# Seven block products for all columns of both output projections

## The chip, the cores and the metric

The kernel runs on one core of a Trainium2 chip. The metric is device time in microseconds (us): the median of three runs of the same program was 2065.28 us (2064.89 to 2066.32). A profile of one more execution shows what each engine did: PE is the matrix engine (PEld its weight loads), DVE the vector engine, ACT the scalar engine, POOL the general engine, SP the engine that issues most plain loads. Partition means one of the 128 rows of on-chip memory; PSUM is the memory that matrix products are summed in, in banks of 128 x 512 numbers.

## The reference

Two residual layers over x (512 tokens x 2048 columns, float32):

```
x = x + (attention(norm(x)) * silu(gate)) @ da_w_out      # layer 0, 8 heads
x = x + (rwkv(norm(x))      * silu(gate)) @ rw_w_out      # layer 1, 32 heads in 16 pairs
```

Both output projections are matrix products of 512 x 2048 by 2048 x 2048. This case is about these two alone. Every product is done in float32 precision by three passes: each factor is split into a high part (a cast) and a low part (the rest), and high x high, high x low and low x high are summed (`mm3`, L116).

## The kernel before

**Tiling.** K (the 2048 channels that are summed over) has 16 tiles of 128, the tokens 4 tiles of 128, the output columns 4 blocks of 512. One product (one instruction of PE) takes a 128 x 128 tile of the activations and a 128 x 512 tile of the weights. The activations of one K tile are a "row" (128 channels x 512 tokens); `split_row` (L471) casts it on ACT (L475) and takes the low part on DVE (L476). `split_w` (L92) does the same for weights, one K tile at a time: ACT L109, DVE L110. High and low weight tiles have four buffers each, raw weights (two K tiles, 512 KB) three, named wraw.

**Order.** The program is written as one sequence; a planner orders it for each engine by priority and by when it takes things to be ready, and inserts the waits. `split_w` runs at a raised priority, the chains below at a higher one. Each engine, and each queue of transfers, then works strictly in its order. Transfers issued by SP are plain loads; those that add into on-chip memory are issued by POOL.

**Output stage of layer 0.** Column blocks 0 and 1 are plain (`unit_tok`, L184): for each pair of K tiles, 2 x 4 token tiles x 3 passes = 24 products. Beside block 0 the last head's attention still runs. It is a `Chain`: a sequence of steps that `tick` (L168) advances by one whenever a given number of products has been issued. Its last step makes the last two rows (K tiles 14 and 15); `feed` loads and splits the other rows a little ahead of their use. The attention of one 128-token block is scores, `turn` (transposition), `weigh`, `turn_y`; four blocks overlap. Beside block 1, `sum_forms` (L758) loads rows of the first 12 K tiles again and makes four sums of them (below).

Column blocks 2 and 3 go through `seven` (L793). It takes 12 of the 16 K tiles as two halves of 6, the tokens as two halves of 256 and the columns as two blocks of 512, and does the 2 x 2 x 2 block product by seven block products in place of eight (the scheme of Strassen and Winograd). Each block product is 3 groups of two K tiles, 12 products a group, 36 in all. It needs sums of activations (S1 to S4, made by `sum_forms`) and sums of weights. The weights are summed in place: `add_w` (L788) lets POOL issue a transfer that adds another block's weights to the ones on the chip, once they are split. Three such tiles, Ts, live through the whole function: 11 uses them first, then S1, S2 and 22. The weights of S4 (b22) are changed in place in the same way for S3. The remaining 4 K tiles are added plainly (`plain`).

The order of `seven` is 11, 12, plain pairs on the first columns, S1, first plain pair on the second columns, S2, S4, second plain pair on the second columns, S3, 22. The banks are named X (11, S2, S3), y and z. The residual x is loaded by SP before the sums; `take` (L824) adds a bank to it on DVE (L827; in the plain blocks L1058 and L1852).

**Output stage of layer 1.** The same, from L1804 on. Beside block 0 run the scan of the last head pair (steps of 4, 4 and 5 products) and the end of the pair before. After the scan come `outputs` (L1671, L1675: tile Y), `centre`, `normal` (L1696 to L1704), and `finish_y` (four transpositions, L1716, and L1718), then the gate (L1592) and the split of row 15. Row 14 comes from the pair before.

Of the kernel before, what the change touches and what calls it, by code (L numbers as in the profile page):

```python
# [13 lines left out]
F32 = mybir.dt.float32  # L14
# [9 lines left out]
P = 128  # L24
# [728 lines left out]
NS = 6  # L753
KG = 2
PLACES = {"11": (0, 0), "12": (0, 1), "21": (1, 0), "22": (1, 1)}


def sum_forms(g, src, i, rows, homes):  # L758


    nc = g.nc
    for r, k0 in zip(rows, (i * KG, NS + i * KG)):
        nc.gpsimd.dma_start(out=r, in_=src[k0 * P : (k0 + KG) * P, :].rearrange("(k p) t -> p k t", p=P))
    (a, b), (c, d) = [(r[:, :, 0:256], r[:, :, 256:512]) for r in rows]
    out = {}
    for nm, o, x, y, op in (("S1", d, b, d, ALU.subtract), ("S3", b, a, b, ALU.subtract),
                            ("S2", d, d, a, ALU.subtract), ("S4", c, c, d, ALU.add)):
        with g.tc.issue_after(g.rowsplit):
            nc.vector.tensor_tensor(out=o, in0=x, in1=y, op=op)
        tags = homes[i][nm]  # L770
        n = KG if len(tags) < 2 * KG else 1
        if len(tags) == 1:
            pool, t, m = tags[0]
            both = pool.tile([P, 2, n, 256], F32R, name="f" + nm, tag=t, bufs=m)
            at = [both[:, 0], both[:, 1]]
        else:
            at = [x[0].tile([P, n, 256], F32R, name="f" + nm, tag=x[1], bufs=x[2])[:] if type(x) is tuple else x
                  for x in tags]
        out[nm] = []
        for x in range(KG // n):  # L780
            hi, lo, v = at[2 * x], at[2 * x + 1], o[:, x * n : (x + 1) * n]
            nc.scalar.copy(hi, v)
            nc.vector.tensor_sub(lo, v, hi.bitcast(F32))
            out[nm] += [(hi[:, k], lo[:, k]) for k in range(n)]
    return out
# [7 lines left out]
def seven(g, w, load, rows, sums, c1, c2, acc, Ts, banks, done, begin=None):  # L793
# [3 lines left out]
    nc = g.nc  # L797

    def products(out, lhs, wt, first, end):
        for k in range(KG):  # L800
            for t in range(2):
                aH, aL = lhs(k, t)
                mm3(nc, out[t][:], aH, aL, wt[0][:, k, :], wt[1][:, k, :], first and k == 0, end and k == KG - 1,
                    g, True)

    def block(k0, t0):
        return lambda k, t: [x[:, t0 + t * P : t0 + (t + 1) * P] for x in rows[k0 + k]]

    def prod(out, i, form, raw, first=False, end=False):
        wt = split_w(g, None, KG, 512, 0, raw)  # L810
        if form in PLACES:
            t, kb = PLACES[form]
            lhs = block(kb * NS + i * KG, t * 256)
        else:
            lhs = lambda k, t: [x[:, t * P : (t + 1) * P] for x in sums[i][form][k]]
        products(out, lhs, wt, first, end)

    def plain(i, c, *outs):
        k0 = 2 * NS + i * KG
        wt = split_w(g, None, KG, 512, 0, load(k0, c))  # L820
        for out, t0, first, end in outs:
            products(out, block(k0, t0), wt, first, end)

    def take(nm, ps, op=ALU.add):  # L824
        with g.tc.high_priority(offset=SCAN):
            for t in range(2):
                nc.vector.tensor_tensor(out=acc[nm][t], in0=acc[nm][t], in1=ps[t][:], op=op)  # L827

    N = NS // KG
    last = N - 1  # L830
    X, y, z = banks(0), banks(1), banks(2)
    for i in range(N):
        load_w(g, Ts[i], w[c1 // 512], i * KG, slice(0, KG))
# [1100 lines left out]
```

## Time and profile before

| | us |
|---|---|
| median of 3 runs | 2065.28 (2064.89 to 2066.32) |
| the profiled execution | 2065.58 |
| its span, first to last instruction | 2063.5 |
| PE busy | 2048.4 (99%) |
| DVE busy | 1676.3 (81%) |
| ACT busy | 1276.0 (62%) |
| POOL busy | 417.8 (20%) |

An instruction's row has its start and its length in us, the engine, the line of the kernel (L118 is line 118), the operation, the tiles out<-in, and in square brackets how long the engine was idle before it and what ended that. A row of a stretch has its borders, its length, and each engine's busy time. Matrix products overlap in the profile: one lasts 0.39 us, but the next starts earlier. Issuing, branch and semaphore instructions do not count as busy.

### The profile page before, as it was taken

Reading aid. Unit: us, or ns where it says so; the run is one execution under the profiler, and the core shown is the slowest. Engines: PE = TensorE matmul, PEld = TensorE weight load, DVE = VectorE, ACT = ScalarE, POOL = GpSimd, SP = SyncE. Lnnn points to the kernel's source line nnn. Section 1 sums busy time; section 2 is a strip of 40 time slices with the busy share of each in tenths; the row PEclk is TensorE's granted clock in tenths of the full one; section 3 lists DMA queues with packets and bytes.
Section 4 is the critical chain, followed back from the end, with each engine's and each line's share of the span. In section 5 each row is a group of like instructions: output and inputs, shape, how many; then the busy total and the mean of one; then the engine's idle time right before and its main releaser. Section 6 shows DMA issues by size and latency. Waiting matters only on the chain. (4 is left out here: it accounts for less than half of the span.)

```text
span 2063.5 us, 35254 instructions
## 1 busy us (share of the span) xinstructions
PE 2048.4 (99%) x11924; PEld 1689.0 (82%) x11924; DVE 1676.3 (81%) x4379; ACT 1276.0 (62%) x3043; POOL 417.8 (20%) x733
## 2 busy tenths in 40 slices
PE   9999999999999999999999999999999999999999
PEld 8878878888888888888778888888888888877887
DVE  5979798897978976576878888888888888887745
ACT  5667676776767754455666666666666666665433
POOL 0020211202111000101233322222333213232001
PEclk9999999999999999999999999999999999999999
DMA  6387877869688665742222222222222222244665
GB/s 203 114 166 184 167 169 167 179 172 177 172 161 217 171 200 187 179 114 95 75 75 70 82 77 81 76 87 75 78 76 80 70 89 74 84 134 151 214 165 121
DMA packets 100773, 269.70 MB, mean 131 GB/s; under 512 B 12432, under 2 KB 28960, under 8 KB 100592
## 3 DMA queue, kind: packets, MB, share of 16 engines
q1 hardware_dynamic: 62016, 173.21, 26.3%
q0 software_dynamic: 24144, 78.23, 20.8%
q10 hardware_dynamic: 14432, 16.01, 2.2%
q8 instruction: 94, 1.54, 0.3%
q14 instruction: 87, 0.71, 0.1%
HBM read 251.41 MB, written 15.99 MB: 130 GB/s over the span
## 5 line engine op out<-in xcount | busy, mean ns | idle before, releaser
L118 PE MATMUL pp<-hH,wh 128*128 128x512 f32 x1024 | 416.6, 407 | 0.0
L118 PE MATMUL pp<-hL,wh 128*128 128x512 f32 x1024 | 411.9, 402 | 0.0
L118 PE MATMUL pp<-hH,wl 128*128 128x512 f32 x1024 | 411.7, 402 | 0.0
L109 ACT CAST wh<-wraw 128x512 fp32r<-128x512 f32 (+1 forms) x412 | 254.3, 618 | 221.7 <-PE pp L118 128.8
L110 DVE TENSOR_TENSOR wl<-wraw,wh 128x512 fp32r<-128x512 f32 (+1 forms) x412 | 292.6, 711 | 83.2 <-ACT wh L109 77.7
L118 PE MATMUL pp<-wh,hH 128*128 128x512 f32 x820 | 325.1, 397 | 0.4 <-DVE G L382 0.4
L118 PE MATMUL pp<-wl,hH 128*128 128x512 f32 x820 | 321.8, 392 | 0.6 <-DVE wl L616 0.6
L118 PE MATMUL pp<-wh,hL 128*128 128x512 f32 x820 | 321.3, 392 | 0.0
L118 PEld LDWEIGHTS pp<-hH,wh 128*128 128x128 f32 x1024 | 192.8, 188 | 38.0 <-issue 2.1
L118 PEld LDWEIGHTS pp<-hH,wl 128*128 128x128 f32 x1024 | 193.1, 189 | 33.2
L118 PEld LDWEIGHTS pp<-hL,wh 128*128 128x128 f32 x1024 | 193.1, 189 | 31.4
L118 PE MATMUL pp<-wh,S 128*128 128x512 f32 x672 | 214.5, 394 | 0.0
L615 ACT CAST wh<-T 128x512 fp32r<-128x512 f32 x224 | 137.1, 621 | 94.2 <-PE pp L118 71.0
L118 PEld LDWEIGHTS pp<-wh,hH 128*128 128x128 f32 x820 | 154.0, 188 | 32.3 <-issue 0.6
L118 PEld LDWEIGHTS pp<-wh,hL 128*128 128x128 f32 x820 | 154.5, 188 | 31.4
L1633 POOL COPY SA<-VS 64x64 f32<-64x64 f32 x224 | 75.1, 335 | 518.2 <-DVE VS L1651 464.6
L118 PEld LDWEIGHTS pp<-wl,hH 128*128 128x128 f32 x820 | 154.2, 188 | 30.7 <-DVE wl L616 0.9
L616 DVE TENSOR_TENSOR wl<-T,wh 128x512 fp32r<-128x512 f32 x224 | 150.5, 686 | 25.4 <-ACT wh L615 24.8
L588 POOL DMA_DIRECT2D T<-in_da_w_in_dram x84 | 72.1, 858 | 388.5 <-DMA wraw<-in_da_w_in_dram 193.9
L1498 DVE SCALAR_TENSOR_TENSOR tmpl<-LT,n,Tm 128x60 f32<-128x60 f32 (+24 forms) x496 | 135.6, 273 | 13.3
L118 PEld LDWEIGHTS pp<-wh,S 128*128 128x128 f32 x672 | 124.7, 188 | 24.7 <-ACT wh L615 0.4
L118 PE MATMUL pp<-wl,S 128*128 128x512 f32 x336 | 132.2, 393 | 0.2 <-DVE wl L616 0.2
(377 smaller groups left out, 4015.3 us busy)
## 6 DMA issues: line engine op xcount, KB each, us to landing
wraw<-in_rw_w_in_dram SPq DMA_DIRECT2D x128, 512.0 KB, 3.6
T<-in_da_w_in_dram POOLq DMA_DIRECT2D x84, 512.0 KB, 6.4
wraw<-in_da_w_in_dram SPq DMA_DIRECT2D x64, 512.0 KB, 4.1
T<-in_da_w_in_dram SPq DMA_DIRECT2D x28, 512.0 KB, 4.4
wraw<-in_da_w_out_dram SPq DMA_DIRECT2D x26, 512.0 KB, 4.5
wraw<-in_rw_w_out_dram SPq DMA_DIRECT2D x26, 512.0 KB, 4.1
wraw<-in_da_w_in_dram POOLq DMA_DIRECT2D x21, 512.0 KB, 6.8
yr<-yd SPq DMA_DIRECT2D x22, 256.0 KB, 3.6
```

What stands on the lines that cost most here:

```text
L109: nc.scalar.copy(hi[:], raw[:, k : k + n])
L110: g.split = nc.vector.tensor_sub(lo[:], raw[:, k : k + n], hi[:].bitcast(F32)).ins
L118: m = nc.tensor.matmul(out, a, b, start=s, stop=e, skip_group_check=skip)
L588: self.g.nc.gpsimd.dma_start(out=raw, in_=src, accum_op=ALU.add)
L615: g.nc.scalar.copy(hi[:], raw[:, k])
L616: g.nc.vector.tensor_sub(lo[:], raw[:, k], hi[:].bitcast(F32))
L1498: st = nc.vector.scalar_tensor_tensor(tt, LT[:, i : i + 1, i + 1 :].to_broadcast([P, s, n]), n2[:, i : i + 1], Tm[:, 0:s, i : i + 1].to_br ...
L1633: nc.gpsimd.tensor_copy(p.SA[r_, c - 1, :], VS[r_, c, h, :])
```

## The change

All four column blocks of both projections go through the block products, as two pairs of blocks (columns 0 and 1, columns 2 and 3), with the same 12 of 16 K tiles. The four plain K tiles are now tiles 6, 7, 14 and 15 (`PLAIN`), and the halves are tiles 0 to 5 and 8 to 13 (`FIRST`).

- A class `Blocks` holds one pair; `outputs_of` sets the order. First come the products that need no sums: 12 of both pairs in turns, with a plain pair of K tiles (6 and 7) each, then 11 of the first pair. These are 132 products, and `feed` is called along them (`pace`). Then `finish` issues the rest of the chain that makes the last rows. Then `one.rest`: plain pairs on the first columns (6, then 14), S1, both plain pairs on the second columns, S2, S4, S3, 22. Then 11 of the second pair and its `rest`.
- The four sums are loaded along the first products and made one kind at a time (`Forms.make`): S1 after `finish`, S2, S4 and S3 inside `one.rest`. The second pair uses the same sums.
- The residual is no longer loaded ahead. `Blocks.copy` copies the first partial sum of each output block from PSUM on ACT, and POOL issues a transfer that adds x (or layer 1's input) to it, 256 KB at a time, 16 times a layer. `take` adds the later partial sums on DVE.
- In layer 1 the end of the pair before is issued at n of 10 in place of 6; rows 14 and 15 are split in `last_rows`, which is called after the 132 products.
- Raw weights other than Ts use the three wraw buffers alone. Homes of several tiles change.

```
+FIRST = {0: 8, 1: 0}
+PLAIN = (6, 14)
...
+    def copy(self, nm, ps, sign=1.0):
+        nc, (t, c) = self.g.nc, PLACES[nm]
+        with self.g.tc.high_priority(offset=SCAN):
+            for i in range(2):
+                nc.scalar.activation(self.acc(nm)[i], ps[i][:], AF.Copy, scale=sign)
+                r0 = (2 * t + i) * P
+                nc.gpsimd.dma_start(out=self.acc(nm)[i], accum_op=ALU.add,
+                                    in_=self.x[r0 : r0 + P, self.c1 + c * 512 : self.c2 + c * 512])
...
+    def first12(self, i, bank):
+        if not i:
+            self.y = self.banks(bank)
+        if i < NS // KG:
+            self.prod(self.y, i, "12", self.load(FIRST[1] + i * KG, self.c1), i == 0)
+        else:
+            self.plain(PLAIN[0], self.c1, (self.y, 0, False, True))
+            self.copy("11", self.y)
+
+    def rest(self, begin=None, then=lambda nm: None):
...
+        self.plain(PLAIN[0], c1, (z, 256, True, False))
+        self.plain(PLAIN[1], c1, (y, 0, True, True), (z, 256, False, True))
+        self.take("11", y)
+        self.done("11")
+        self.copy("21", z)
+        then("S2")
+        y, z = self.banks(1), self.banks(2)
+        for i in range(N):
+            self.prod(y, i, "S1", Ts[i], i == 0, i == last)
+            add_w(g, Ts[i], w, FIRST[1] + i * KG, c2)
+        self.copy("22", y)
+        then("S4")
+        for n, k0 in enumerate(PLAIN):
+            self.plain(k0, c2, (z, 256, n == 0, n == 1), (y, 0, False, False))
+        self.take("22", z)
+        for i in range(N):
+            self.prod(X, i, "S2", Ts[i], end=i == last)
+            add_w(g, Ts[i], w, FIRST[1] + i * KG, c1)
+        self.copy("12", X, -1.0)
+        then("S3")
+        b22 = []
+        for i in range(N):
+            b22.append(self.load(FIRST[1] + i * KG, c2)[:])
+            self.prod(y, i, "S4", b22[i], end=i == last)
+            add_w(g, b22[i], w, FIRST[0] + i * KG, c2)
+        self.take("12", y)
+        self.done("12")
+        for i in range(N):
+            self.prod(X, i, "S3", b22[i], end=i == last)
...
+def outputs_of(g, one, two, feed, finish, begin=None):
+    def pace(n):
+        feed(4 + n // 2, g.m)
+    N, s = NS // KG, 0
+    for i in range(N + 1):
+        for x, (b, bank) in enumerate(((two, 0), (one, 1))):
+            pace(s)
+            b.first12(i, bank)
+            s += KG
+        if i == 1:
+            one.sums.load(0)
     for i in range(N):
+        pace(s)
+        pace(s + 1)
+        one.first11(i)
+        s += KG
+        if i:
+            one.sums.load(i)
+    finish(g.m)
+    one.sums.make("S1")
+    one.rest(then=one.sums.make)
     for i in range(N):
+        two.first11(i)
+    two.rest(begin)
...
-            if n >= 6 and not q.done:
+            if n >= 10 and not q.done:
```

288 lines of the change are left out of this document (123 added, 165 removed).

## The prediction

> **What bounds the kernel now.** I read the head of the profile first, then the table of stretches cut at the borders of the two output stages, then single instructions inside them.
>
> ```profile
> span 2063.5 us, 35254 instructions
> PE 2048.4 (99%) x11924; PEld 1689.0 (82%) x11924; DVE 1676.3 (81%) x4379; ACT 1276.0 (62%) x3043; POOL 417.8 (20%) x733
> ...
> 726.20:766.60 40.40, 40.12 (x203) 32.70 (x202) 32.09 (x107) 23.16 (x57) 0.76 (x1) 1.00 0.56 184
> 766.60:826.10 59.50, 58.95 (x268) 48.50 (x267) 37.70 (x73) 26.28 (x53) 4.50 (x6) 1.00 0.60 192
> 826.10:906.10 80.00, 80.00 (x357) 66.14 (x356) 50.78 (x93) 37.48 (x71) 9.66 (x13) 1.00 0.71 164
> 1882.80:1922.30 39.50, 39.42 (x274) 31.90 (x274) 25.97 (x64) 22.24 (x59) 11.76 (x23) 1.00 0.56 174
> 1922.30:1979.40 57.10, 57.10 (x255) 47.27 (x254) 36.42 (x66) 19.75 (x33) 0.95 (x1) 1.00 0.55 173
> 1979.40:2058.40 79.00, 79.00 (x348) 64.94 (x347) 44.41 (x68) 29.84 (x48) 9.36 (x11) 1.00 0.68 156
> ```
>
> Behind each stretch and its length stand the busy times of PE, PEld, DVE, ACT and POOL, then the granted clock (1.00) and the DMA share. Three rows belong to the output stage of each layer: the first 132 products of the first column block, the rest of the two plain blocks, and the seven block products. PE is idle for under 1 us in all six together. So a product less is worth its spacing, and every new wait of PE is paid in full.
>
> ```profile
> 815.20 0.39 PE L118 MATMUL pp<-wh,hL 128*128 128x512 f32 x1
> ...
> 818.82 0.39 PE L118 MATMUL pp<-wh,hH 128*128 128x512 f32 x1
> ```
>
> These are start and length of one instruction; the second is 16 products behind the first: 3.62 / 16 = **0.226 us** a product (the 0.39 is latency, which overlaps).
>
> **What the change takes away.** A plain column block is 16 K tiles x 4 token tiles x 3 passes = 192 products, so two are 384. Two blocks in the new way are 7 x 6 x 2 x 3 = 252, and 4 K tiles x 4 x 2 x 3 = 96 for the plain rest: 348. That is 36 fewer in each layer, 72 in all: 72 x 0.226 = **16.3 us**. The rest of the sum is what PE may now wait for.
>
> **Work that is added off PE.** Each pair of blocks casts 52 weight tiles (six each for seven products, four for the first plain tiles, which are now loaded twice, two and four for the others), each layer 104 where it was 32 + 50 = 82. Residual adds leave DVE (8 a layer) and 28 partial sums stand where 14 stood.
>
> ```profile
> L109 ACT CAST wh<-wraw 128x512 fp32r<-128x512 f32 (+1 forms) x412 | 254.3, 618 | 221.7 <-PE pp L118 128.8
> L110 DVE TENSOR_TENSOR wl<-wraw,wh 128x512 fp32r<-128x512 f32 (+1 forms) x412 | 292.6, 711 | 83.2 <-ACT wh L109 77.7
> ...
> L110 DVE TENSOR_TENSOR wl<-wraw,wh 128x512 fp32r<-128x512 f32 x12 | 8.2, 687 | 2.8 <-ACT wh L109 2.8
> ```
>
> The 22 casts cost ACT 22 x 0.62 = 13.6 us and DVE 22 x 0.69 = 15.2 us a layer (0.687 in the last row, which counts the first stretch only). DVE also gets 6 sums (4.1 us), ACT 16 copies of PSUM (the nearest row is the cast's 0.62: 9.9 us). In layer 0 DVE then works 120.6 + 19.3 = 140 of some 172 us, so on the mean it hides behind PE. Not everywhere: 132 products now need 22 tiles in the first stretch where 12 were cast, 32.09 + 10 x 0.69 = 39 of 40.4 us. The four forms are now made behind it, in bursts of 3 x 3 instructions, instead of beside a plain block. Four tiles are cast ahead (four buffers), which is 24 products or 5.4 us of cover now and was 48. Bounds for PE's waits from DVE in both layers 0 to 4 us (the 2 x 2 us by which 39 plus a burst of 6 x 0.69 on DVE exceed 40.4); I take **1.0**, since DVE full from 710 to 730 left PE busy there:
>
> ```profile
> 715.00:720.00 5.00, 5.00 (x24) 4.14 (x23) 5.00 (x16) 4.18 (x10) 0.00 (x0) 1.00 0.98 354
> 725.00:730.00 5.00, 5.00 (x26) 3.83 (x24) 5.00 (x12) 4.69 (x12) 0.00 (x0) 1.00 1.00 358
> ```
>
> **The third tile of layer 0.** The stage begins at about 726.2: the last head's first key transposition is queued 6 products ahead of its end.
>
> ```profile
> 724.23 0.60 PE L361 MATMUL pt<-ident,t 128*128 128x128 f32 x4
> ...
> 726.42 0.61 ACT L109 CAST wh<-wraw 128x512 fp32r<-128x512 f32 x1
> ...
> 730.53 0.69 DVE L110 TENSOR_TENSOR wl<-wraw,wh 128x512 fp32r<-128x512 f32 x1
> ```
>
> The third tile is cast by ACT at 726.42 but reaches DVE at 730.53, behind the head's last conversions, and is done at 731.2. Now PE wants it 24 products in; afterwards 12 products (2.7 us) and two transpositions in, at 729.6. Wait 1.6 us; bounds 0 (another order on DVE) and 2; I take **1.2**.
>
> **The last two rows, the largest new wait.** K tiles 14 and 15 come from the chain that runs beside the stage, one step per so many products. Until now PE first needed them 168 products in; now after 132 products the rest of the chain is issued at once, 12 plain products (tile pair 6) follow, and then pair 14 is wanted at 144. Nothing else can fill in: the next products (S1) need the bank that pair 14 sums into.
>
> ```profile
> 737.99 0.22 PE L118 MATMUL sc<-qkT 128*128 128x128 f32 x1
> ...
> 769.70 0.28 PE L118 MATMUL o<-V,al 128*128 128x256 f32 x1
> ...
> 774.34 0.41 PE L446 MATMUL yt<-ident,G 128*128 128x128 f32 x2 [0.24 <-DVE G L441]
> ...
> 775.95 1.30 DVE L476 TENSOR_TENSOR hL<-Tt,hH 128x512 fp32r<-128x512 f32 x2 [0.47 <-ACT hH L475]
> ```
>
> In layer 0 the first scores (737.99) stand 46 products into the stage, the last weighting 92 steps later: 138 by its own pace, so at 132 by the new order. It ends at 769.98; the first of the two rows is split at 776.6, that is 6.6 us of square, root, scale, transposition, cast. PE has 12 products (2.7 us) and the transpositions (0.4) for it: wait 3.5; bounds 2 and 5 (by DVE's share), I take **3.5**.
>
> ```profile
> 1882.84 0.39 PE L118 MATMUL pp<-wh,hH 128*128 128x512 f32 x1
> ...
> 1915.68 1.20 PE L1671 MATMUL Y<-VS,G 128*64 128x64 f32 x32
> ...
> 1925.24 0.69 DVE L1704 TENSOR_TENSOR yc<-yc,rsg 128x512 f32<-128x512 f32 x1
> ...
> 1927.99 0.60 PE L1716 MATMUL pt<-ident,yc 128*128 128x128 f32 x4
> ...
> 1931.26 0.69 DVE L476 TENSOR_TENSOR hL<-mixE,hH 128x512 fp32r<-128x512 f32 x1 [0.69 <-ACT hH L475]
> ```
>
> In layer 1 the stage begins at 1882.84. The last pair's outputs (Y) start at 1915.68, 110 products in by their gaps and some 123 by time; I take 120. They end 1.8 us later; tile 15 is split 14.5 us after that, 2.1 of them waiting for PE's turn: 12.4, or 9.9 with DVE's other work taken out. Pair 14 first needs tile 15 at product 150, 30 products (6.8 us) and 0.4 us on. Wait between 0.5 (Y at 110, 9.9) and 5.2; I take **3.2**. The step moved from n of 6 to 10 (another head pair's end) is not late: its row waits for 144 too.
>
> **S3 straight behind S4.** S3 uses S4's weights after a DMA has added to them in place. Now the second plain pair (24 products) stands between; afterwards nothing does.
>
> ```profile
> 874.58 0.86 POOL L790 DMA_DIRECT2D wraw<-in_da_w_out_dram  x1 [1.87 <-DVE wl L110]
> 877.74 0.86 POOL L790 DMA_DIRECT2D wraw<-in_da_w_out_dram  x1 [2.30 <-DVE wl L110]
> ...
> 883.59 0.39 PE L118 MATMUL z<-wh,hH 128*128 128x512 f32 x1
> ...
> q0 software_dynamic: 1054, 3.79, 72.0%
> ...
> wraw<-in_da_w_out_dram POOLq DMA_DIRECT2D x3, 512.0 KB, 5.9
> ```
>
> The plain pair starts at 883.59, where S3 would. The additions land 5.9 us after issue: the second at 883.6, cast by 885.0, wanted one group (2.7 us) into S3, 886.3. That fits by 1.3. But a residual add of 2 x 256 KB now enters POOL's queue between the first and the second: the copy of S2's sum ends about 1.5 us into S4. The queue row (860 to 890 us) gives 0.72 x 30 / 3.79 = 5.7 us a MB, 3.0 us for 524 KB, if an addition of x costs what one of weights does. Then the second lands at 886.6, cast by 888.0: wait 1.7, and the third is in time. Bounds 0 and 3.2 (x half as dear again, since its pieces are half as long); I take 1.2, four times: **4.8**. The other additions have 36 products or more.
>
> The Trainium skill (DMA: Bandwidth & Descriptors, SWDGE vs HWDGE vs iDMA) says that accumulating transfers are issued from GpSimd alone and that a single software queue is allocated. That speaks against the change: the new residual adds cannot go round the weight adds; the trace agrees as far as all of these stand in q0.
>
> **Sum.** -16.3 + 1.0 + 1.2 + 3.5 + 3.2 + 4.8 = **-2.6**. Removed residual loads are worth nothing: SP's queue did not hold PE. The profiled execution took 2065.58 us (span 2063.5, 2.1 around it), 0.3 over the median of 2065.28; so the forecast for the median is **2062.7**.
>
> **The rivals.** *The waits are hidden:* additions land in time, DVE keeps up, the third tile comes earlier, and only the two row waits are paid: 2065.3 - 16.3 + 6.7 = **2055.7**. For it: the 1.3 us of room at S3, PE undisturbed at a full DVE. Against: the residual adds stand in the same queue.
>
> *POOL's queue turns it round (slower):* per pair 12 weight additions (36 us), four of x (12) and 15 loads; the loads cost 524 KB at the 356 GB/s of a full stretch, 1.5 us each, 22 in all. That is 70 of 79 us, where the share was 0.71.
>
> ```profile
> 2059.00:2060.00 1.00, 0.82 (x4) 0.35 (x2) 0.83 (x2) 0.00 (x0) 0.00 (x0) 1.00 0.00 0
> ...
> 2061.00:2061.50 0.50, 0.00 (x0) 0.00 (x0) 0.00 (x0) 0.00 (x0) 0.00 (x0) 1.00 0.98 356
> 2061.50:2062.00 0.50, 0.00 (x0) 0.00 (x0) 0.00 (x0) 0.00 (x0) 0.00 (x0) 0.85 1.00 381
> 2062.00:2062.50 0.50, 0.00 (x0) 0.00 (x0) 0.00 (x0) 0.00 (x0) 0.00 (x0) 0.50 0.30 111
> ```
>
> If an x addition takes 4.5 us, each S3 waits 3.2 (12.8), and casts of the first stage, whose loads share the engines with the forms' loads, lose 2 in each layer: -16.3 + 8.9 + 12.8 + 4 = +9.4, **2074.7**. It decides from 2.9 us at each S3: (16.3 + 4.1 - 8.9) / 4. For it: DMA at 0.98 to 1.00 around 715 to 730 already. Against: the queue must stay full from S2 on.
>
> *The clock falls in the row waits:* the rows just shown are the end of the kernel. PE stops at 2059.8, and the granted clock is 1.00 until about 2061.9, then 0.50. A row wait of 3.5 us could do the same; at half clock for as long as from that stop to the end (3.7 us) each costs 1.9: 2062.7 + 3.7 = **2066.4**. The Trainium skill (TensorE: Matmul & The Clock Gate, Part 1) puts the fall at one idle window of about 3.4 us, free running; the 2 us seen here are a shorter one.
>
> **How the numbers follow.** Forecast 0.40, with its own range 2058 to 2067 (each wait by half its bounds); hidden 0.30; queue 0.18; clock 0.12. A measurement of this kernel tells about 0.2% (4.1 us) from no change, so faster means below 2061.1 and slower above 2069.4. Faster: 0.28 of the hidden case and a third of the forecast, 0.42. Slower: 0.17 of the queue, 0.04 of the clock, 0.02 of the forecast, 0.23. The rest, 0.35, is the same. Range 2053 to 2073.
>
> **What would show it.** PE idle some 3 to 4 us once in each layer, 30 to 40 us into its output stage, at pair 14 and released by the row's split; idle of 1 to 2 us at the second group of S3, four times, released by a DMA on the weights; 1.2 us at the third tile. Products 0.226 apart elsewhere. PE busy 16 us less would confirm the count. The forecast is wrong if the row waits are gone (the planner found other work), if S3 starts without a gap, or if PE waits for weight loads in the first stage.

## The result, and the profile after

| | before | after |
|---|---|---|
| median, us | 2065.8 (2064.9 to 2066.5) | 2122.7 (2119.6 to 2125.2) |
| span of the profiled execution | 2063.5 | 2123.1 |
| ratio after / before | | 1.0275 (95%: 1.0257 to 1.0293) |

The changed kernel is 57 us slower; the forecast was 2062.7 with a range of 2053 to 2073. First the head of the profile of after, with the work of each engine; this execution took 2125.2 us, the longest of the four.

```profile
span 2123.1 us, 35355 instructions
PE 2054.2 (97%) x11852; PEld 1686.2 (79%) x11852; DVE 1698.9 (80%) x4423; ACT 1317.8 (62%) x3119; POOL 471.3 (22%) x789
```

The 72 products are gone (11924 to 11852), and still PE is busy 5.8 us longer. PE's idle time rose from 15.1 to 68.9 us, by 53.8. So the span's 59.6 us are -16.3 for the products, +53.8 of waiting, and +22.1 by which the products that are left took longer.

The next row is from the view of tile pp: count, shortest, median and longest duration in ns, and the start of the first and the last. These 1024 products are layer 1's projections, between the two output stages. First before, then after:

```profile
L118 PE MATMUL pp<-hH,wh x1024: 387/393/507, 936.5 to 1882.2; 128*128 128x512 f32 x171
```

```profile
L118 PE MATMUL pp<-hH,wh x1024: 387/393/507, 966.1 to 1911.5; 128*128 128x512 f32 x171
```

Up to the end of layer 0's output stage 29.6 us were lost, in layer 1's (from the last of them to the end) 30.3, and what lies between took the same time. Of the first, some 2.9 us were lost just ahead of the stage. There PE waited for the weighted values (G) of the head before the last, while DVE stood before the first sum of S1 (L780), whose rows were still landing. The last head's first key transposition came at 727.10, before at 724.23. From 650 to 700 PE had been busy all the time before; now it was busy 46.93 of the 50 us.

```profile
689.24 0.41 PE L446 MATMUL yt<-ident,G 128*128 128x128 f32 x2 [1.96 <-DVE G L441]
```

```profile
687.01 0.69 DVE L780 TENSOR_TENSOR frow<-frow 128x512 f32<-128x512 f32 x1 [2.80 <-DMA frow<-yd]
```

The stretches that lost it, in the table of windows of after (borders, length, busy us of PE, PEld, DVE, ACT and POOL, granted clock, DMA share, GB/s):

```profile
773.90:800.40 26.50, 7.61 (x26) 6.18 (x26) 15.06 (x45) 6.95 (x16) 0.88 (x1) 0.55 0.30 77
800.40:842.40 42.00, 42.00 (x185) 34.32 (x183) 17.62 (x26) 18.05 (x32) 11.99 (x14) 1.00 0.82 160
842.40:845.10 2.70, 0.04 (x1) 0.00 (x0) 0.00 (x0) 0.64 (x2) 0.00 (x0) 0.95 1.05 253
...
915.70:918.60 2.90, 0.03 (x1) 0.04 (x1) 0.05 (x1) 0.70 (x2) 0.00 (x0) 1.00 0.99 227
...
1949.20:1957.60 8.40, 0.00 (x0) 0.00 (x0) 1.90 (x3) 2.81 (x7) 1.34 (x3) 0.80 0.82 177
...
1972.40:1988.90 16.50, 7.69 (x21) 5.91 (x22) 11.09 (x22) 5.26 (x9) 1.83 (x3) 0.59 0.27 60
...
2026.60:2029.00 2.40, 0.10 (x2) 0.03 (x1) 0.04 (x1) 0.69 (x2) 0.00 (x0) 1.00 1.05 258
...
2099.70:2102.90 3.20, 0.00 (x0) 0.00 (x0) 0.01 (x1) 0.66 (x2) 0.00 (x0) 1.00 0.92 175
```

Between these places PE is nearly as full as before (42.00 of 42.00 in the second row). Three kinds of place are left; their waits of PE are 47.3 of the 53.8 us. Smaller ones (1.4 us for the chain at 746.5, 2.1 us at 1916.9 in layer 1) were not followed up.

**1. Layer 0, 774 to 800.** Rows of PE, then of DVE and POOL, of after:

```profile
741.50 0.22 PE L118 MATMUL sc<-qkT 128*128 128x128 f32 x1
...
787.70 0.66 PE L446 MATMUL yt<-ident,G 128*128 128x128 f32 x2 [13.78 <-DVE G L441]
...
794.81 0.66 PE L446 MATMUL yt<-ident,G 128*128 128x128 f32 x2 [3.89 <-DVE G L441]
796.69 0.79 PE L118 MATMUL pp<-wh,hH 128*128 128x512 f32 x1 [1.22 <-ACT hH L475]
...
797.71 0.63 PE L118 MATMUL pp<-wh,hH 128*128 128x512 f32 x1
798.14 0.63 PE L118 MATMUL pp<-wl,hH 128*128 128x512 f32 x1
```

```profile
775.88 0.15 DVE L70 SCALAR_TENSOR_TENSOR rs_i<-rs_t,rs_i 128x1 f32<-128x1 f32 x1
781.70 0.69 DVE L780 TENSOR_TENSOR Tt<-Tt 128x512 f32<-128x512 f32 x1 [5.67 <-DMA Tt<-yd]
782.31 0.15 DVE L67 TENSOR_TENSOR rs_t<-rs_i 128x1 f32<-128x1 f32 x1
...
787.07 0.48 DVE L441 SCALAR_TENSOR_TENSOR G<-o,ro,G 128x256 f32<-128x256 f32 x1
```

```profile
771.57 0.74 POOL L770 DMA_DIRECT2D Tt<-yd  x1 [0.47 <-ACT Tt L450]
```

PE waits for G, the last head's weighted values. Its square root (L63 to L70) is half done at 775.9; the next instruction in DVE's order is a sum for S1 (L780) whose rows POOL could ask for only at 771.6, since their home Tt was in use by row splits until then. They land 10 us later, and DVE stands still with PE's only work behind it. The first scores of the chain were also 3.5 us later than before (741.50, 737.99), 2.9 of it lost ahead of the stage, and its rounds took longer. From the first scores to the third weighting it was 23.98 us before, 29.05 in after, and 28.88 in the first experiment below, with DVE (the third busy time) nearly full:

```profile
737.99:761.97 23.98, 23.70 (x118) 19.17 (x117) 19.41 (x77) 14.08 (x37) 0.76 (x1) 1.00 0.39 119
```

```profile
741.50:770.55 29.05, 27.41 (x136) 22.09 (x134) 27.21 (x93) 23.18 (x54) 6.97 (x9) 1.00 0.80 186
```

```profile
738.84:767.72 28.88, 27.39 (x136) 22.12 (x134) 27.14 (x93) 23.02 (x54) 7.52 (x9) 1.00 0.81 191
```

So two rounds, not one, were left at product 132: hence the second wait of 3.9.

**2. Layer 1, 1949 to 1989.** The last read of TT by the scan (PE), the load of it (SP), its cast (ACT) and the product that needs it (PE):

```profile
1948.32 0.33 PE L1691 MATMUL sm<-rhs,TT 128*128 128x64 f32 x2
...
1957.63 0.80 PE L118 MATMUL pp<-wh,hH 128*128 128x512 f32 x1 [8.46 <-ACT wh L109]
...
1978.52 1.12 PE L1769 MATMUL pt<-ident,yc 128*128 128x128 f32 x4 [6.13 <-DVE yc L1757]
1982.33 0.79 PE L118 MATMUL pt<-wh,hH 128*128 128x512 f32 x1 [2.69 <-ACT hH L475]
```

```profile
1948.71 0.33 SPq L76 DMA_DIRECT2D TT<-in_rw_w_out_dram  x1
```

```profile
1956.96 1.14 ACT L109 CAST wh<-TT 128x512 fp32r<-128x512 f32 x2 [3.23 <-DMA TT<-in_rw_w_out_dram]
```

The second tile of Ts lies in TT, which the scan still reads; the load can start at 1948.7 and lands 8.2 us later. Before, Ts was first used after the scan. The waits of 6.1 and 2.7 for row 15 then have largely the same cause as in layer 0 (a sum waited 3.7 us for its rows at 1973.75).

**3. S3 behind S4, four times** (2.69, 2.89, 2.30, 3.23 us; 11.1 in all). Rows of POOL around the first:

```profile
830.54 0.85 POOL L801 DMA_DIRECT2D wraw<-in_da_w_out_dram  x1 [1.84 <-DVE wl L110]
831.83 0.86 POOL L842 DMA_DIRECT2D xq<-in_x_dram  x1 [0.44 <-ACT xq L840]
834.59 0.84 POOL L842 DMA_DIRECT2D xq<-in_x_dram  x1 [1.90 <-issue]
838.36 0.88 POOL L801 DMA_DIRECT2D wraw<-in_da_w_out_dram  x1 [2.93 <-issue]
```

The residual additions stand between the first and the second weight addition, as the prediction had it; the second is issued 7.8 us behind the first, and its cast starts at 844.46, 2.4 us after PE ran out of products.

### The profile page after: what moved, and what is told of

Its sections match the earlier page's. It is cut to its first block, busy times and chain, and to the rows that moved or that the text cites. A ratio compares the mean times of both kernels' runs of the same rounds, so it can differ in the third digit from the quotient of the medians.

```text
span 2123.1 us, 35355 instructions
## 1 busy us (share of the span) xinstructions
PE 2054.2 (97%) x11852; PEld 1686.2 (79%) x11852; DVE 1698.9 (80%) x4423; ACT 1317.8 (62%) x3119; POOL 471.3 (22%) x789
## 5 line engine op out<-in xcount | busy, mean ns | idle before, releaser
L118 PE MATMUL pp<-wh,hH 128*128 128x512 f32 x696 | 278.0, 400 | 12.2 <-ACT wh L109 8.5
L118 PE MATMUL pp<-wl,hH 128*128 128x512 f32 x696 | 275.4, 396 | 0.8 <-DVE wl L616 0.6
L118 PE MATMUL pp<-wh,hL 128*128 128x512 f32 x696 | 273.8, 394 | 0.0
L118 PEld LDWEIGHTS pp<-wh,hH 128*128 128x128 f32 x696 | 131.5, 189 | 40.5 <-ACT wh L109 8.9
L118 PEld LDWEIGHTS pp<-wl,hH 128*128 128x128 f32 x696 | 131.7, 189 | 26.8 <-DVE wl L110 1.1
L118 PEld LDWEIGHTS pp<-wh,hL 128*128 128x128 f32 x696 | 131.8, 190 | 26.6
```

Source lines behind the costliest of these rows:

```text
L118: m = nc.tensor.matmul(out, a, b, start=s, stop=e, skip_group_check=skip)
```

## Experiments

All times are medians; the kernel before, run beside them, took 2065.2 to 2065.8 us.

### Sums behind the last row

```diff
-            nc.vector.tensor_tensor(out=o, in0=x, in1=y, op=op)
+            with self.g.tc.issue_after(self.g.rowsplit) if nm == "S1" and i == 2 else ExitStack():
+                nc.vector.tensor_tensor(out=o, in0=x, in1=y, op=op)
```

> The change, with one order altered: the S1 sums of the third pair of K tiles (the pair whose rows land late) may go to DVE only behind the split of the last row, in both layers. Theory (DVE works in order and stands still for late rows, with the chain of the last row behind it): in layer 0 PE's wait for the chain's tile G falls from 13.8 us to about 4, and both such waits together from 17.7 to 7 or 8; in layer 1 the wait for yc falls from 6.1 to 2 or 3; the granted clock falls less around both. The time goes from 2122.7 to 2098 to 2110. Rival (the chain is that long by itself, the sums only fill its waiting): the waits stay within 3 us and the time is 2119 to 2126. Rival (the wait only moves): G comes early, but PE then waits 8 us or more at the third group of S1 for its sums; time 2114 to 2122.

2111.3 us (2110.1 to 2117.8): 11.4 less. PE's waits in layer 0's stage (us in total, times, longest):

```profile
PE yt L446 <- DVE G L441: 10.2, 3, 6.1
PE pp L118 <- ACT wh L109: 8.3, 2, 4.7
```

The late sums were 7.5 of the 17.7 us there, and the wait for yc in layer 1 is gone. But 10.2 us for G stay, more than expected: that much the chain, with its longer rounds, is too long for its cover. In layer 1 the row's split still cost PE 1.8 us.

### 11 apart from TT

```diff
...
+        raw = self.Ts[i]
+        if self.apart and i == 1:
+            raw = self.load(FIRST[0] + i * KG, self.c1)
         load_w(self.g, self.Ts[i], self.w[self.c1 // 512], FIRST[0] + i * KG, slice(0, KG))
-        self.prod(self.X, i, "11", self.Ts[i], i == 0, i == NS // KG - 1)
+        self.prod(self.X, i, "11", raw, i == 0, i == NS // KG - 1)
...
+        two[0].apart = True
```

> The change, with one buffer altered: in layer 1 the second group of 11 of the first pair takes its weights from a raw buffer, and the tile TT that the scan of the last head pair still reads is loaded behind that (one load of 512 KB more). Theory (the load of TT waits for the scan's last read at 1948.3 and lands 8.2 us later): the 8.5 us wait of PE at 1949 falls under 1 us, and what follows comes earlier by as much; with the clock that fell in it the time goes from 2122.7 to 2110 to 2115. Rival (the last row's chain sets the end of that stretch anyway): the 6.1 us wait for yc grows by what is won, and the time is 2120 to 2125.

2125.1 us (2122.4 to 2128.4), no gain: the rival. The wait for TT is gone and the next one in line has grown:

```profile
PE pt L1774 <- DVE yc L1762: 10.2, 1, 10.2
```

### S3 last

```diff
+        z = self.banks(2)
+        for i in range(N):
+            self.prod(z, i, "22", Ts[i], i == 0, i == last)
+        self.take("21", z)
         for i in range(N):
+            if i == last and begin:
+                begin(g.m)
             self.prod(X, i, "S3", b22[i], end=i == last)
         self.take("22", X, ALU.subtract)
         self.done("22")
         self.take("21", X)
-        z = self.banks(2)
-        for i in range(N):
-            if i == last and begin:
-                begin(g.m)
-            self.prod(z, i, "22", Ts[i], i == 0, i == last)
-        self.take("21", z)
```

> The change, with the last two block products of each pair exchanged: 22 stands between S4 and S3 (36 products), S3 is last. Theory (the in-place additions on the weights of S4 have too little cover): the four waits of 2.3 to 3.2 us between S4 and S3 (11.1 us together) are gone, none over 0.5 us takes their place, and with the clock that falls after two of them the time goes from 2122.7 to 2106 to 2112. Rival (the transfers as a whole are too many, DMA share 0.9 to 1.05 in these stretches): waits of PE for weights of the same sum stand elsewhere behind S4, time 2117 to 2124.

2110.6 us (2108.0 to 2113.2): 12.1 less, within the theory's range. No wait between S4 and the next product is left; the one wait for weights of layer 1 is that for TT (8.6). One of 1.9 us, for an addition on DVE (L848), is new, against the expectation's 0.5.

### No residual additions

```diff
                 nc.scalar.activation(self.acc(nm)[i], ps[i][:], AF.Copy, scale=sign)
-                r0 = (2 * t + i) * P
-                nc.gpsimd.dma_start(out=self.acc(nm)[i], accum_op=ALU.add,
-                                    in_=self.x[r0 : r0 + P, self.c1 + c * 512 : self.c2 + c * 512])
```

> The change without the 32 transfers that add x (or layer 1's input) to the copied partial sums: the residual is left out of the result, everything else is the same. Theory of the prediction (two of them stand between the first and the second weight addition in POOL's queue): the second weight addition of S3 is issued about 5 us earlier (in layer 0 at some 833 of 838.4), the four waits before S3's second group fall under 0.5 us each, and the time goes from 2122.7 to 2106 to 2112. Rival (an addition needs that long by itself): the waits stay at 2 us or more, time 2119 to 2124.

This kernel leaves x out of its result. 2098.7 us (2095.5 to 2099.1): 24.0 less, above the theory's 11 to 17. The weight additions of the first S4 now follow each other at 3.3 and 2.2 us, and the four waits are gone:

```profile
826.33 0.85 POOL L801 DMA_DIRECT2D wraw<-in_da_w_out_dram  x1 [1.82 <-DVE wl L110]
829.59 0.86 POOL L801 DMA_DIRECT2D wraw<-in_da_w_out_dram  x1 [2.40 <-DVE wl L110]
831.82 0.84 POOL L801 DMA_DIRECT2D wraw<-in_da_w_out_dram  x1 [1.38 <-DVE wl L110]
```

The other half came where I had not looked: the wait for TT fell from 8.5 to 4.0 and those for G from 17.7 to 14.5. That the additions of x delay the other transfers of the crowded stretch too is the likely reason; it is not shown transfer by transfer.

### The three edits together

The diffs of "Sums behind the last row", "11 apart from TT" and "S3 last" in one kernel.

> The change with the three edits before together: sums of the third pair behind the last row's split, 11's second group in layer 1 from a raw buffer, S3 last. Theory (each wait stands by itself, and the wait for TT was only hidden behind late sums when it was taken away alone): 2122.7 less 11.4, less 12.1, less the 8.5 of TT with its clock: 2088 to 2093, no wait for TT over 1 us at about 1940, the wait for yc not over 2 us. Rival (the last row's chain of layer 1 sets the end of its stretch whatever the weights do): the third edit gives nothing, 2097 to 2102, and the wait for yc or for row 15's split grows to 8 us or more.

2095.2 us (2090.6 to 2095.4), a little above the theory's range: the edit that gave nothing alone gives 4 here, if the other two add up (2122.7 - 11.4 - 12.1 = 2099.2). In layer 1 the rows' own waits are left:

```profile
PE pt L118 <- ACT hH L475: 4.7, 1, 4.7
...
PE pt L1775 <- DVE yc L1763: 1.6, 1, 1.6
```

### Filling products in the waits

```diff
+        m = None
+        for _ in range(110 if t == 2 and yT is not None else 0):
+            with g.tc.issue_after(m) if m else ExitStack():
+                m = nc.tensor.matmul(pt[:, 256:384], g.ident[:], g.ident[:], start=True, stop=True).ins
```

> The change with 110 products of 128 x 128 more on PE, about 11.5 us, in the 13.8 us that PE waits for the chain's tile G in layer 0; nothing uses their result. Theory (an idle PE loses its clock, and the loss is part of the time): the granted clock stays at 1.00 from 774 to 786, the 12 products of the weighting after it take some 1.6 us where they took 2.9, the products behind the wait are 0.23 us apart where they were 0.43; the time goes from 2122.7 to 2116 to 2120. Rival (the vector engine's chain sets the time there, the clock costs nothing): 2121 to 2125, with the wait before the next tile G longer by what the weighting gains.

2130.7 us: a product of this shape is two records of 0.112 us, so they took 24.8 us in a wait of 13.8. The kernel lost 8.0 us of the 11.0 by which they were too long. The clock was 1.00 through this wait, and the weighting behind them took 1.5 us instead of 2.9. With 54 such products and 15 in the wait that follows:

```diff
...
-        for _ in range(110 if t == 2 and yT is not None else 0):
+        for _ in range({2: 54, 3: 15}.get(t, 0) if yT is not None else 0):
```

> The change with filling products in the two waits of PE for the chain's tile G in layer 0, their number mended: 54 (two records of 0.112 us each, 12.1 us) in the wait of 13.8 us and 15 (3.4 us) in the one of 3.9; nothing uses their result. Theory (the idle waits cost the clock, and that costs time): granted clock 1.00 from 774 to 800, the weighting between the two waits takes 1.5 us where it took 2.9, the first plain products behind the second wait are 0.23 us apart where they were 0.43; together 3.5 us, 2122.7 becomes 2117 to 2121. Rival (the clock falls after such a long wait in any case, or the chain on the vector engine takes it back): 2122 to 2126.

2122.2 us (2118.5 to 2126.2): not to be told from 2122.7. From the transposition of G before the waits to S1's first product it is 31.0 us (773.91 to 804.88) where it was 33.7 (770.38 to 804.03), so the clock was worth 2.7 us there; the total is blurred by the other waits (S3's here 3.4, 1.9, 3.4, 3.1).

### Another order for the first pair

What the waits have in common is that row 14 is wanted at product 144. In this kernel S1 comes first and the plain tiles of the first columns last; the sums of layer 0 use the rows 8 to 13 that already lie in Tt; S3 is last.

```diff
+    def rest_late(self, finish, then):
+        then("S1")
+        for i in range(N):
+            self.prod(y, i, "S1", Ts[i], i == 0, i == last)
...
+        finish(g.m)
+        self.copy("22", y)
+        then("S2")
+        then("S4")
+        for n, k0 in enumerate(PLAIN):
+            self.plain(k0, c2, (z, 256, n == 0, n == 1), (y, 0, False, False))
...
+            self.prod(X, i, "S2", Ts[i], end=i == last)
...
+            self.prod(y, i, "S4", b22[i], end=i == last)
...
+            self.prod(z, i, "22", Ts[i], i == 0)
...
+            self.prod(X, i, "S3", b22[i], end=i == last)
...
+        self.plain(PLAIN[0], c1, (z, 256, False, False))
+        self.plain(PLAIN[1], c1, (y, 0, True, True), (z, 256, False, True))
...
-    sums = Forms(g, g.yd, ((sx[0], sx[1]), (sx[2], Tt[:, 6:8]), (Tt[:, 0:2], Tt[:, 2:4])), homes)
+    sums = Forms(g, g.yd, ((Tt[:, 2:4], sx[0]), (Tt[:, 6:8], sx[1]), (Tt[:, 0:2], sx[2])), homes, (0,))
```

> The change with another order for the first pair: S1 stands directly behind the 132 first products, then the plain tiles of the second columns (row 14 is wanted at product 192), S2, S4, 22, S3, and the plain tiles of the first columns last; in layer 0 the sums are made from the rows 8 to 13 that are on the chip already, so that half of their loads and all late ones fall away; S3 is last in the second pair too; in layer 1 the first pair's 12 stands ahead of the second's. Theory (the row waits come from row 14 being wanted at 144, the late loads from their homes): no wait for G over 1 us in layer 0, its output stage under 190 us (209.3 in the change); in layer 1 the wait for TT of about 8 us stays, and a wait for the third sums of S1 of 2 to 6 us behind it; time 2072 to 2085. Rival (DMA share of 0.9 and over: the additions for S1 come 36 products behind 11 in place of 72 and are late): waits at S1's groups of 2 us or more in both layers, time 2085 to 2100.

2074.5 us (2071.8 to 2076.8): 48.2 less than the change. Several things change at once here, and no run splits the 48.2 us among them. Layer 0's stage is back to what it was before (the 1024 products start at 937.0), and layer 1 keeps the wait for TT:

```profile
PE pp L118 <- ACT wh L109: 8.2, 1, 8.2
```

The next kernel was to take that away:

> The kernel with the other order for the first pair (S1 directly behind the first products, plain tiles of the first columns last, sums from rows on the chip in layer 0), and 11's second group in layer 1 from a raw buffer. Theory (TT is wanted before the scan has read it): the wait of about 8 us at 11's second group is gone, but S1's second group wants TT 36 products later with another block added: a wait of 2 to 5 us there; time 3 to 8 us under the same kernel without this edit, 2066 to 2080. Rival (TT is free too late for S1 as well): the wait moves whole to S1's second group, and the time is within 2 us of that kernel.

Its switch was never set, so it is the kernel before it once more (2074.9 us) and says nothing on its question. The next one does: layer 1's sums from the rows on the chip too, T1 in a half of G1 that is free by then.

```diff
...
-        Ts = [flat(x) for x in g.TT] + [g.low.tile([P, KG, 512], F32, name="T2", tag="SX", bufs=3)[:]]
+        Ts = [flat(g.TT[0]), early[:, 1]] + [g.low.tile([P, KG, 512], F32, name="T2", tag="SX", bufs=3)[:]]
```

> The kernel with the other order for the first pair (row 14 wanted at product 192, S3 last, plain tiles of the first columns at the end), and now in layer 1 too the sums are made from the rows 8 to 13 where their splits read them, so half of the rows' loads and the late ones fall away; the second weight tile T1 is a buffer that nothing else uses by then, not the tile TT of the scan. Theory (what is left against the kernel before is the wait for TT, 8.2 us, with the clock that fell in it and the late sums behind it): no wait over 2 us in layer 1's output stage, 2074.5 becomes 2060 to 2066. Rival (the DVE, with 18 more small sums, or the chain of the last row takes the place): waits of 3 us or more for a split or for yc at products 180 to 192 of layer 1, time 2067 to 2074.

2068.2 us (2064.1 to 2070.6): 6.3 less. The largest wait of layer 1's stage is 1.8 us, for yc, as the theory had it, but the time lies in the rival's range: layer 0 lost 5.5 us to waits for splits there, the subject of the next section. With all residuals loaded plainly instead of added by transfer:

```diff
+            self.g.nc.gpsimd.dma_start(out=self.acc(nm)[i],
+                                       in_=self.x[r0 : r0 + P, self.c1 + c * 512 : self.c2 + c * 512])
...
-                nc.scalar.activation(self.acc(nm)[i], ps[i][:], AF.Copy, scale=sign)
...
+                a = self.acc(nm)[i]
+                nc.vector.tensor_tensor(out=a, in0=a, in1=ps[i][:], op=ALU.add if sign > 0 else ALU.subtract)
```

> The kernel with sums from rows on the chip in both layers, and the residual is loaded plainly by POOL ahead of each first partial sum, which DVE then adds (16 additions a layer more on DVE, 16 copies fewer on ACT, no accumulating transfer of x). Theory (each residual addition holds the queue of the weight additions for longer than a plain load): waits for weights behind S2 and S4 get less, DMA share falls; 1 to 5 us under the same kernel with residual additions, 2057 to 2065. Rival (once S3 is last and nothing is late, POOL's queue holds nobody up, and DVE has more to do in the first stage): the same within 1 us, or up to 4 us slower.

2067.8 us (2065.6 to 2072.2), the rival's "same": once S3 is last, the additions of x cost no more than DVE's work for them.

### One instruction on DVE

What was left in layer 0 were two additions on DVE (`take`) to a tile in which a transfer of x was still landing, with weights behind them. One I took away by loading x of block 21 ahead, the other (11) I moved behind S1.

```diff
-        if i == NS // KG - 1:
+        if i == NS // KG - 1 and not late:
             self.take("11", self.X)
...
         self.copy("22", y)
+        self.take("11", X)
...
+        self.fetch("21")
...
-        self.copy("21", X)
+        self.take("21", X)
```

> The kernel with sums from rows on the chip in both layers and row 14 wanted at product 192, with two edits more in the first pair: the residual of block 21 is loaded plainly ahead of the 22 products (its first partial sum is then added on DVE), and 11's sum is added to its partial result behind S1 instead of ahead of it. Theory (the wait of 3.3 us at 841 in layer 0 comes from an addition of x that stands directly between two partial sums of 21, and the one of 2.0 at 768 from a DVE that adds 11 while S1's weights wait): both fall under 1 us, with the clock behind them; 2068.2 becomes 2058 to 2064, under the 2065.8 of the kernel before. Rival (DVE is full to 770 whatever is moved; the wait at 768 stays, others come up as 21's residual load takes POOL's queue): 2064 to 2069, no difference from the kernel before that can be measured.

2065.7 us (2062.2 to 2068.4), the rival's range and not to be told from the kernel before. The wait at 841 is gone. The addition of 11 had been written later but kept its place in DVE's order, so the wait for S1's weights grew:

```profile
PE pp L118 <- DVE wl L110: 4.0, 2, 3.8
```

Put behind S1's weights by an explicit order, and then, with `g.rowsplit` for `g.split`, behind the last row:

```diff
-        self.take("11", X)
+        with g.tc.issue_after(g.split):
+            self.take("11", X)
```

> The same kernel as before it (residual of block 21 loaded plainly, row 14 wanted at product 192), but the addition of 11's sum now stands in DVE's order behind the low parts of S1's weights; in the run before it had kept its place ahead of them. Theory (DVE stands still from 764.8 to 767.3 because its next instruction adds to a tile in which a residual addition is still landing, and the low parts of S1's first weights stand behind it): the wait of 3.8 us at 768.7 in layer 0 falls under 1 us and the clock does not fall behind it; 2065.7 becomes 2058 to 2062.5. Rival (the weights of S1 are late by their own additions): a wait of 2.5 us or more for the weights stays there, 2063.5 to 2067.

> The same kernel, with the addition of 11's sum now behind the split of the last row on DVE (behind S1's weights alone it stood ahead of the last head's chain, and PE waited 5.2 us for G in place of 3.8 us for weights). Theory (that one DVE instruction, waiting for its residual transfer, is all that holds layer 0 up between 760 and 780): no wait over 1.2 us in layer 0's output stage; 2066.6 becomes 2058 to 2062.5, and the kernel is faster than the one before by 0.15 to 0.35%. Rival (S1's weights or the chain are late by themselves there, DMA share 0.9 and over): one wait of 2.5 us or more between 760 and 790 stays, 2063.5 to 2067.

2066.6 and 2073.5 us. The first is in its rival's range, but not for its reason: PE's wait went from the weights to G (5.2 us). The second is above both ranges: the wait for G stood there in two parts (7.4), and the third weights of S1 were late by their own addition, issued at 762.3 behind four additions of x. So the queue was put in order: x for 11 and 21 behind S1's weight additions.

```diff
+        for b in (self, two):
+            for i in range(2):
+                with g.tc.issue_after(g.added):
+                    b.add_x("11", i)
```

> The same kernel, with the eight additions of x for the two 11 blocks (four in each layer) and the plain load for 21 behind the additions on S1's weights in POOL's queue, where they stood ahead of the last of these; 11's sum is added behind the split of the last row. Theory (the residual additions in POOL's one queue make S1's weights late in layer 0, as they made S3's late in the change): the wait of 3.5 us on DVE for the third weights of S1 and PE's waits for G of 7.4 us fall under 1.5 us together; 2073.5 becomes 2057 to 2063, under the kernel before. Rival (the transfers are late for the amount that is moved in that stretch, DMA share 0.9 and over, whatever their order): a wait of 2.5 us or more between 755 and 790 stays, 2064 to 2072.

2067.1 us (2066.2 to 2068.3), the rival's range. S1 starts without a wait, and the chain's own length shows, later in the stage:

```profile
PE yt L446 <- DVE G L441: 4.1, 1, 4.1
PE z L118 <- ACT hH L475: 1.2, 1, 1.2
```

Last, more cover for it: S2 ahead of the second plain pair, row 14 wanted at 228. The addition of 11's sum goes back ahead of S2.

```diff
-        finish(g.m)
-        with g.tc.issue_after(g.rowsplit):
-            self.take("11", X)
-        for n, k0 in enumerate(PLAIN):
-            self.plain(k0, c2, (z, 256, n == 0, n == 1), (y, 0, False, False))
-        self.take("22", z)
+        self.plain(PLAIN[0], c2, (z, 256, True, False), (y, 0, False, False))
+        with g.tc.issue_after(g.split):
+            self.take("11", X)
...
             self.prod(X, i, "S2", Ts[i], end=i == last)
...
+        finish(g.m)
+        self.plain(PLAIN[1], c2, (z, 256, False, True), (y, 0, False, False))
+        self.take("22", z)
```

> The same kernel with S2 ahead of the second plain pair, so that row 14 is wanted at product 228 in place of 192 (144 in the change), and 11's sum added ahead of S2. Theory (with the queues in order, what is left is the last head's chain: PE waits 4.1 us for G at 782 and 1.2 for the row in layer 0, about 2 in layer 1, and the clock falls behind it): no wait for G, yc or a row over 0.5 us; 2067.0 becomes 2057 to 2063, faster than the kernel before. Rival (DVE is the bound of the first 60 us of the stage, so that whatever is not late for the row is late for S2's sums or weights): a wait of 2.5 us or more for S2's weights or sums between 765 and 790, 2063.5 to 2069.

2061.7 us (2058.5 to 2064.9); against the kernel before 0.9983 (0.9974 to 0.9992): **faster than both**, by 0.17% here, and in the theory's range. The wait for G fell from 4.1 to 1.4 us, not under the 0.5 of the theory; the one for the row is gone. Its head and the same row as above:

```profile
span 2060.0 us, 35348 instructions
PE 2036.1 (99%) x11852; PEld 1675.5 (81%) x11852; DVE 1699.0 (82%) x4438; ACT 1315.6 (64%) x3118; POOL 464.2 (23%) x783
```

```profile
L118 PE MATMUL pp<-hH,wh x1024: 387/393/507, 933.6 to 1879.4; 128*128 128x512 f32 x171
```

PE is busy 12.3 us less than before. Of the 16.3 us, 2.9 are won in layer 0's stage and 0.7 in layer 1's; of the rest, 8.8 are more idle time of PE: pieces under 2 us, and 5.4 us from PE's last product (2054.6) to the end where it was 3.7, since S3 last leaves DVE four additions. In 4.0 the products took longer at a granted clock of 1.00; why is open.

## Why the prediction was wrong

**The count** (-16.3) was right: 72 products fewer, still 0.228 us apart where nothing disturbs (801.29 to 803.80 in after: 11 products in 2.51 us).

```profile
801.29 0.40 PE L118 MATMUL z<-wh,hH 128*128 128x512 f32 x1
...
803.80 0.40 PE L118 MATMUL z<-wh,hL 128*128 128x512 f32 x1
```

That PE's busy time would show it failed: the products that are left took 22.1 us longer, most of it at half clock (below).

**DVE's load in the first stage** (+1.0, bounds 0 to 4) is the step that failed first, in two ways. I counted DVE's work against PE's time, and had the sums "made behind it, in bursts". The first way is order: a sum waited for its rows with the chain behind it, 2.80 us ahead of the stage and 5.67 in it. I never asked when those rows could be loaded (their homes: Tt until row 13 is split, G1 until the scan has ended), though the home of every tile was in the diff. Taking that order away gave 11.4 us. The Trainium skill (TensorE: Matmul & The Clock Gate, Part 1, "Architectural detail") calls ACT and DVE strict first-in, first-out queues; the trace agrees, by the 5.67 us in which DVE stood before one sum. The second way is amount: I had DVE at 39 of 40.4 us and still took 1.0, but beside a nearly full DVE the chain's rounds took 5.1 us longer, and 4.9 with the late sum moved away. That the full DVE stretched them fits the rows; no run isolates it.

**The last two rows** (+3.5 and +3.2): the mechanism was right, the size wrong. With the late sums out of the way PE still waits 10.2 + 1.2 us in layer 0 (forms_behind_rows), and with all three edits 4.7 + 1.6 in layer 1. In layer 0 I took the chain to be at its last step at product 132, by its pace before. With the sums behind the last row its first scores were only 0.85 us late (738.84), but its longer rounds made the third weighting 5.75 us late (767.72, before 761.97), and a whole round of weighting, root and transposition stood behind it.

**Ts in TT** had no term at all. The step "11 first" was costed by products and casts, and no line of the prediction asked who still reads the tile that 11's weights land in: 8.5 us of waiting. Taken away alone it gave nothing (the row's chain took over), with the two other edits 4.

**S3 behind S4** (+4.8, bound 12.8): right in place and cause, 11.1 us in size. I took the second addition to be 3.0 us late for the two additions of x; it was issued 7.8 us behind the first, where it is 3.3 without them, so 4.5. Moving S3 gave 12.1; PE was busy 6.2 us less with it (2048.0), so the half clock behind these waits was part of their price.

**The third tile** (+1.2) did not show: PE was idle for under 0.3 us from 720 to 740. **The removed residual loads** were rightly worth nothing, but the additions that replaced them were priced at S3 alone; leaving them out gave 24.0 us, 12 of it elsewhere.

**The clock** was a rival at 1.9 us for each of two waits. It fell, or was still down, in or shortly behind every wait of 2.1 us and more in the two output stages. PE's busy time in slices of 1 us, times what the granted clock lacks of 1.00, adds up to 17 us (7 in layer 0, 10 in layer 1): an estimate of its price within the 22.1. The last kernel has the same 11852 products at a granted clock of 1.00, and PE is busy 18.1 us less. Only 2.7 us were measured by an edit. **POOL's queue** as a rival had the sign and S3's price (12.8), but not the row waits, which were the larger part.

## What to carry to other kernels

When work is moved earlier, list for each tile it touches who reads that home last and when a load into it can land: here waits of this kind, those at S3 and the half clock behind them turned 16.3 us saved into 57 lost. On an engine that works in order, the cost of an instruction that waits is everything behind it, so a product of little urgency (a sum, an addition to a result) belongs behind the chain that PE waits for, by an explicit order. A wait taken away alone may give nothing because the next one stands right behind it; the gain came only in kernels where the thing that is ready last (row 14) was wanted later, though these changed the sums and the queues as well.

## What the runs showed of the hardware

The clock fell without a long wait. In the run with 54 and 15 filling products PE idled 1.7 of 2.2 us, worked on, and 0.6 us later was at half clock for 3.4 us:

```profile
795.50:797.70 2.20, 0.52 (x4) 0.21 (x3) 0.51 (x2) 1.20 (x4) 0.00 (x0) 1.00 0.00 0
797.70:798.30 0.60, 0.60 (x3) 0.51 (x4) 0.60 (x2) 0.60 (x2) 0.00 (x0) 1.00 0.00 0
798.30:801.70 3.40, 3.40 (x10) 2.63 (x9) 1.63 (x4) 0.37 (x1) 0.00 (x0) 0.52 0.00 0
801.70:805.00 3.30, 3.30 (x16) 2.71 (x15) 1.01 (x2) 2.05 (x6) 0.00 (x0) 0.98 0.21 79
```

The Trainium skill (TensorE: Matmul & The Clock Gate, Part 1) has the clock halved after one idle window of about 3.4 us that runs freely, and full again after one busy window. The 3.4 us at half clock agree with the second; the first does not, as no idle time of 3.4 us came before. The four waits at S3 in after, of 2.30 to 3.23 us, show the same. Their rows above have 0.95 and 1.00 because the clock fell between just before the end of the wait and 1.5 us behind it; PE then ran some 3.4 us at half clock each time (an estimate from the granted clock of short windows). Behind the second:

```profile
920.00:922.00 2.00, 2.00 (x7) 1.49 (x6) 1.55 (x6) 1.97 (x6) 0.00 (x0) 0.50 0.40 139
```

What makes the clock fall at such waits stays open.

POOL stood for 1.9 and 2.9 us ahead of the second addition of x and of the weight addition behind it, waiting for nothing that the trace shows ("issue" in the rows above). Without the additions of x no such gap stands there. Gaps of this kind stand ahead of plain loads of POOL too (3.02 us at 649.89 in after), so they are not shown to belong to additions alone.
